# The sample's queries against its states: states as moving operand in four column groups of the array, queries stationary

## The chip, the cores and the metric

One NeuronCore of a Trainium2 chip runs the whole program. The metric is the device time of one execution in microseconds (us); the time of a kernel is the median of its runs. TensorE is called PE in the profile (PEld is its weight load), VectorE DVE, ScalarE ACT, GpSimd POOL, and SyncE SP.

## What is computed

One inference step of a decoder with two layers. Layer 0 mixes by gated linear attention (GLA), layer 1 by a gated short convolution; each layer has an MLP. There are 1024 prompt tokens and a sample of 8 sequences with 4 new tokens each. Only the GLA of the sample is touched. Each of its 8 sequences brings its own state S (128 x 256) for each of 4 heads. Cut to what matters:

```python
def gla_core(q, k, v, g, s0):      # for the sample: one chunk of 4 tokens per sequence
    b = jnp.cumsum(g, axis=3)
    q_dec = q * jnp.exp(b)
    k_dec = k * jnp.exp(-b)
    scores = jnp.where(causal, jnp.einsum('bhnid,bhnjd->bhnij', q_dec, k_dec), 0.0)
    o_intra = jnp.einsum('bhnij,bhnjv->bhniv', scores, v)
    ...
    o_inter = jnp.einsum('bhncd,nbhdv->bhncv', q_dec, s_prev)   # s_prev: the states brought in
    o = o_intra + o_inter
    # new state: decay * s0 + k^T v
```

The new states and the outputs of all tokens are results, in float32.

## The kernel before

The 1056 tokens (1024 of the prompt, then the 32 of the sample) lie along the free axis in three groups of 384, 384 and 288; the sample is the last 32 columns of group 2. The GLA stage runs over 4 heads. In each head: the projections of queries and keys for three token groups, then `core` over nine token tiles (eight of the prompt, and the ninth is the sample), then the gates and the output projection. `proj` (L241) is 24 matmuls that TensorE runs one after the other (8 slices of the contraction, each in three matmuls of high and low parts, L236 to L238). `gated` (L572) takes one `proj`; there are two for each token group. `out(tg)` (L761) is `accumulate` (L252): 8 output blocks of 6 matmuls, each block in a bank of PSUM of its own.

TensorE's order in this stage is that of the code. Work that follows from a step with some delay is put into a list (`after`, L210) with a due time in a planner's clock that counts matmuls (`cost`, L207); `tick` (L221), called at the end of each `proj` and each output block, runs what is due. `need(key)` runs what must be done now. The orders of DVE, ACT and POOL in this stage are made by a scheduler.

PSUM has eight banks here (`ps()`, L81). A new tile takes a bank whose former tile has been read, and TensorE waits for that.

The ninth tile goes to `sample` (L666). Its steps: `outputs` (L672) is due at the first `tick`, that is behind the first `proj` of the gates. For each of two halves m of the 256 value columns it multiplies the sample's values `vt` with the masked scores `sTs`, and then, for each of 8 sequences, a 128 x 128 slice of the state as stationary operand with 4 query columns as moving operand. In float32 each of these matmuls is two instructions on TensorE. ACT copies the result to `o`, and `rms` begins the normalisation. `products` (L685), 800 ns later in the planner's clock, so behind the next `proj`, forms k^T v of the 8 sequences into four banks (`box`): it uses 32 rows of the array at a time, in four row groups. `state(j)` (L693) then adds on DVE, four operations for each j, and a DMA on POOL's queue stores four states; a bank of `box` is free when the operation of `state(1)` on it is done. The buffers of the states (`raw`, three in all) are later filled by the next weights.

The vectors `seq[:, 0]` and `seq[:, 1]` are scalars for each partition, one or zero, that pick for row 32 g + t of a 128-row tile the sequence g or 4 + g.

Of the kernel before, what the change touches and what calls it, by code (L numbers as in the profile page):

```python
# [9 lines left out]
F32 = mybir.dt.float32  # L10
# [3 lines left out]
ALU = mybir.AluOpType  # L14
PSUM = bass.MemoryType.PSUM

P = 128
# [3 lines left out]
NSEQ = 8  # L21
LSEQ = 4
NS = NSEQ * LSEQ
# [5 lines left out]
DV = 256  # L29
# [28 lines left out]
def hybrid_step(ctx, tc, x_prompt, x_sample, state_gla, state_conv, gla_w_in, gla_w_gate_up, gla_b_gate,  # L58
# [4 lines left out]
    V, A, G, PE = nc.vector, nc.scalar, nc.gpsimd, nc.tensor  # L63
# [13 lines left out]
    def nm(s):  # L77
        count[0] += 1
        return f"{s}{count[0]}"

    def ps():  # L81
        return psp.tile([P, 512], F32, tag="ps", name=nm("ps"))

    def ring():
        return ringp.tile([P, RINGW], F32, tag="ring", name=nm("ring"))
# [6 lines left out]
    ident = const.tile([P, P], F32, name="ident")  # L92
# [15 lines left out]
    gconst = glac.enter_context(tc.tile_pool(name="gconst", bufs=1))  # L108
# [39 lines left out]
    seq = gconst.tile([P, 2], F32, name="seq")  # L148
    V.tensor_add(seq, seq1[:, 0, :], seq1[:, 1, :])
    for g in (2, 3):  # L150
        V.tensor_add(seq, seq, seq1[:, g, :])


    units = []
# [52 lines left out]
    def cost(n, passes):  # L207
        clock[0] += passes * (n / PE_GHZ + 3.0)

    def after(key, *steps):  # L210

        later.append([clock[0] + steps[0][0], key, list(steps)])
# [18 lines left out]
    def mm(out, w, x, start=True, stop=True):  # L231
        PE.matmul(out, w, x, start=start, stop=stop)  # L232
        cost(out.shape[-1], 4)
# [170 lines left out]
    start = ctx.enter_context(ExitStack())  # L404
# [56 lines left out]
    with tc.tile_pool(name="gp", bufs=3) as gp:  # L461
# [85 lines left out]
        def rms(h, tg, o):  # L547
            n = TGS[tg][1]
            box = {}

            def squares():
                box["a"], box["b"] = ring(), ring()
                A.activation(box["a"][:, :n], o[:, 0, :n], AF.Square)
                A.activation(box["b"][:, :n], o[:, 1, :n], AF.Square)
                (V if tg == 2 else G).tensor_add(box["a"][:, :n], box["a"][:, :n], box["b"][:, :n])

            def split():
                box["mean"] = mean_over(box["a"], n)

            def var():  # L560
                box["var"] = box["mean"]()

            def norm():
                rstd = rstd_of(box["var"], n, RMS_EPS, D // DV)
                for m in range(2):
                    ncol = col["norm_g"] + h * 2 + m
                    V.scalar_tensor_tensor(o[:, m, :n], o[:, m, :n], par[:, ncol:ncol + 1], rstd[:, :n],
                                           op0=ALU.mult, op1=ALU.mult)

            after(("rms", tg), (300, squares), (1500, split), (1500, var), (500, norm))  # L570
# [17 lines left out]
        def core(h, qkk, uv, dec, o):  # L588
# [77 lines left out]
            def sample(k2t, st, vt):  # L666

                tg, off = 2, 256
                q_ = qkk[tg][0]
                box = []  # L670

                def outputs():  # L672
                    po = ps()
                    for m in range(2):
                        ms = slice(m * P, (m + 1) * P)
                        mm(po[:, m * NS:(m + 1) * NS], vt[:, ms], st, stop=False)
                        for i in range(NSEQ):
                            c = i * LSEQ
                            mm(po[:, m * NS + c:m * NS + c + LSEQ], s0[i // 4][:, i % 4, ms],
                               q_[:, off + c:off + c + LSEQ], start=False, stop=i == NSEQ - 1)  # L680
                    A.copy(o[tg][:, :, off:off + NS], po[:, :2 * NS].rearrange("p (m t) -> p m t", t=NS))
                    rms(h, tg, o[tg])
                    after(("states",), (STEP, products), *[(STEP, lambda j=j: state(j)) for j in range(2)])

                def products():  # L685

                    box.extend(ps() for _ in range(4))
                    for j in range(2):
                        for g in range(4):
                            gs = slice(g * NS, (g + 1) * NS)  # L690
                            mm(box[g][:, j * DV:(j + 1) * DV], k2t[gs, j * P:(j + 1) * P], vt[gs, :])

                def state(j):  # L693
                    for g in range(4):
                        S = s0[j][:, g, :]
                        V.scalar_tensor_tensor(S, S, dec[:, 16 + 4 * j + g:17 + 4 * j + g],
                                               box[g][:, j * DV:(j + 1) * DV], op0=ALU.mult, op1=ALU.add)
                    nc.gpsimd.dma_start(gla_s[0, 4 * j:4 * j + 4, h].rearrange("s p v -> p s v"), s0[j])

                after(("sample",), (0, outputs))  # L700

            s0 = []
            e = early(0)
            vt = values(0)
            for t in range(9):
                if t == 5:
                    for half in range(2):
                        s0.append(raw().rearrange("p (s v) -> p s v", v=DV))
                        nc.gpsimd.dma_start(s0[half],
                                            state_gla[0, half * 4:half * 4 + 4, h].rearrange("s p v -> p s v"))  # L710
                if t < 8:
                    e_next = early(t + 1)
                    vt_next = values(t + 1)
                if t == 7:
                    issue()
                    issue()
                if t < 8:
                    chunks(t, *e, vt)
                    if t == 7:
                        nc.gpsimd.dma_start(gla_p[0, 0, h], state["S"])  # L720
                else:
                    sample(*e, vt)
                if t in (2, 5):
                    rms(h, t // 3, o[t // 3])
                e, vt = e_next, vt_next
# [698 lines left out]
```

## Time and profile before

| | us |
|---|---|
| median of 3 runs (lowest, highest) | 2283.0 (2279.68, 2283.72) |
| the profiled execution | 2281.98 |
| its span, first to last instruction | 2280.3 |
| TensorE busy in it | 2204.7 (97%) |
| DVE, ACT, POOL busy | 1629.4, 1140.2, 520.8 |
| mean granted clock of TensorE | 0.980 of full speed |

The span is the time from the first to the last instruction of the profiled execution; 1.7 us lie around it. Busy shares are averages over the whole span; what a stage waits for is read from that stage. A matmul's shown duration reaches past the start of the next one, since matmuls are pipelined: what one costs in a row of them is the distance between starts.

### The profile page before, as it was taken

To read this page: it belongs to the slowest core of one execution; us is meant where nothing else is said; L and a number is where in the kernel's file an instruction comes from. 1 tells how busy PE (TensorE), PEld (TensorE's weight loads), DVE (VectorE), ACT (ScalarE), POOL (GpSimd) and SP (SyncE) were. 2 spreads that over 40 slices of the span, in tenths; PEclk is the share of its full clock that TensorE was granted. 3 is DMA by queue.
4 is the path that set the end of the run, shared out by engine and by line. 5 is a ranking of instruction groups with operands and counts; after the bars stand their busy time and mean duration, and the time that the engine had idled before them with its cause. 6 is when DMAs were issued, how large, how long until landed. Compare 5 with 4: busy or idle time off the path is not lost.

```text
span 2280.3 us, 43300 instructions
## 1 busy us (share of the span) xinstructions
PE 2204.7 (97%) x17341; PEld 2180.1 (96%) x17341; DVE 1629.4 (71%) x3030; ACT 1140.2 (50%) x2083; POOL 520.8 (23%) x547
## 2 busy tenths in 40 slices
PE   9999999997999999999999999988999999999995
PEld 8999999997999999999999999988999999999995
DVE  7464848466688755588788787987578865578875
ACT  4444435258563436554468454446854344664442
POOL 5102321222312022412102313210332111422121
PEclk9999999998999999999999999999999999999997
DMA  5021212114769356868445657640886544868535
GB/s 163 25 74 40 74 32 65 38 58 108 95 123 222 103 93 130 116 134 205 106 76 85 117 117 129 139 109 19 131 138 158 149 109 102 111 120 207 143 78 136
DMA packets 296326, 249.43 MB, mean 109 GB/s; under 512 B 15316, under 2 KB 238648, under 8 KB 296124
## 3 DMA queue, kind: packets, MB, share of 16 engines
q0 software_dynamic: 122624, 106.53, 30.7%
q1 hardware_dynamic: 173500, 140.13, 20.7%
q8 instruction: 136, 2.23, 0.4%
q14 instruction: 66, 0.54, 0.1%
HBM read 224.91 MB, written 9.12 MB: 103 GB/s over the span
## 4 chain that ended last, share of the span: by engine, by line
PE 89%; DVE 5%; DMA 2%; issue 2%; ACT 1%; POOL 0%; SPq 0%; DVEq 0%; ACTq 0%; POOLq 0%
PE pq L865 67%; PE ps L236 6%; PE ps L237 6%; PE ps L238 6%; PE ps L232 3%; DMA SB<-in_mlp_w_down 1%; PE pq L1170 1%; PE pq L1197 1%; DMA SB<-in_conv_w_out 1%; DVE H L1271 1%; DVE bl L848 0%; DVE wl L848 0%; DVE stats L1153 0%; ACT big L1189 0%; DVE Z L334 0%
## 5 line engine op out<-in xcount | busy, mean ns | idle before, releaser
L865 PE MATMUL pq<-bh,wh 128*128 128x264 f32 x4160 | 846.6, 285 | 9.1 <-ACT bh L847 7.1
L865 PE MATMUL pq<-bl,wh 128*128 128x264 f32 x4160 | 846.9, 284 | 2.6 <-DVE bl L848 2.6
L865 PE MATMUL pq<-bh,wl 128*128 128x264 f32 x4160 | 844.3, 285 | 1.8 <-DVE wl L848 1.7
L865 PEld LDWEIGHTS pq<-bh,wh 128*128 128x128 f32 x4160 | 645.4, 189 | 11.1 <-ACT bh L847 9.3
L865 PEld LDWEIGHTS pq<-bl,wh 128*128 128x128 f32 x4160 | 645.5, 189 | 3.4 <-DVE bl L848 3.1
L865 PEld LDWEIGHTS pq<-bh,wl 128*128 128x128 f32 x4160 | 645.4, 189 | 2.6 <-DVE wl L848 2.4
L847 ACT CAST wh<-raw 128x512 fp32r<-128x512 f32 x312 | 193.6, 621 | 393.1 <-PE pq L865 375.0
L848 DVE TENSOR_TENSOR wl<-raw,wh 128x512 fp32r<-128x512 f32 x312 | 214.2, 687 | 125.9 <-ACT wh L847 124.1
L854 POOL DMA_DIRECT2D SB<-in_mlp_w_up x128 | 163.5, 1332 | 424.1 <-DMA SB<-in_mlp_w_up 251.4
L847 ACT CAST wh<-SB 128x512 fp32r<-128x512 f32 x208 | 128.6, 618 | 239.0 <-PE pq L865 217.6
L848 DVE TENSOR_TENSOR wl<-SB,wh 128x512 fp32r<-128x512 f32 x208 | 142.7, 686 | 87.1 <-ACT wh L847 87.1
L847 ACT CAST bh<-H 128x528 fp32r<-128x528 f32 (+1 forms) x292 | 165.4, 570 | 52.3 <-PE pq L865 46.8
L848 DVE TENSOR_TENSOR bl<-H,bh 128x528 fp32r<-128x528 f32 (+1 forms) x292 | 179.2, 625 | 13.0 <-ACT bh L847 12.6
L854 POOL DMA_DIRECT2D SB<-in_mlp_w_down x96 | 85.0, 1155 | 255.4 <-DVE wl L848 138.4
L236 PE MATMUL ps<-XH,whi 128*128 128x384 f32 (+1 forms) x384 | 128.4, 334 | 0.2 <-ACT XH L401 0.2
L237 PE MATMUL ps<-XL,whi 128*128 128x384 f32 (+1 forms) x384 | 127.4, 332 | 0.3 <-DVE XL L402 0.3
L238 PE MATMUL ps<-XH,wlo 128*128 128x384 f32 (+1 forms) x384 | 127.1, 331 | 0.0
L865 PE MATMUL pq<-bh,rh 128*128 128x264 f32 x320 | 95.5, 299 | 21.8 <-ACT rh L847 12.5
L854 POOL DMA_DIRECT2D SB<-in_conv_w_in x48 | 61.2, 1285 | 170.3 <-DMA SB<-in_conv_w_in 73.1
L865 PE MATMUL pq<-bl,rh 128*128 128x264 f32 x320 | 92.9, 291 | 0.0
L865 PE MATMUL pq<-bh,rl 128*128 128x264 f32 x320 | 92.6, 292 | 0.3 <-DVE rl L848 0.2
L962 ACT ACTIVATE H<-H 128x528 f32<-128x528 f32 x96 | 61.9, 645 | 46.9 <-DVE H L982 27.9
(275 smaller groups left out, 3651.4 us busy)
## 6 DMA issues: line engine op xcount, KB each, us to landing
raw<-in_mlp_w_down SPq DMA_DIRECT2D x160, 256.0 KB, 3.1
SB<-in_mlp_w_up POOLq DMA_DIRECT2D x128, 256.0 KB, 4.8
raw<-in_mlp_w_up SPq DMA_DIRECT2D x96, 256.0 KB, 3.0
SB<-in_mlp_w_down POOLq DMA_DIRECT2D x96, 256.0 KB, 7.9
SB<-in_mlp_w_up SPq DMA_DIRECT2D x64, 256.0 KB, 3.8
raw<-in_gla_w_in SPq DMA_DIRECT2D x24, 512.0 KB, 3.8
SB<-in_conv_w_in POOLq DMA_DIRECT2D x48, 256.0 KB, 4.7
raw<-SB POOLq DMA_DIRECT2D x36, 256.0 KB, 4.1
```

The source lines that it names most:

```text
L232: PE.matmul(out, w, x, start=start, stop=stop)
L236: PE.matmul(out, wh, xh, start=first, stop=False)
L237: PE.matmul(out, wh, xl, start=False, stop=False)
L238: PE.matmul(out, wl, xh, start=False, stop=last)
L847: A.copy(hi[:, :w], src)
L848: V.tensor_sub(lo[:, :w], src, f32(hi[:, :w]))
L854: queue.dma_start(dst, src, **kw)
L865: PE.matmul(out[:, c:c + NT], w, b[:, n * NT:(n + 1) * NT], start=first and i == 0, stop=last and i == 2)
L962: A.activation(h, h, AF.Relu, scale=sign)
L1170: PE.transpose(pt[:tn, k * P:(k + 1) * P], z[:, k, t0:t0 + tn], ident)
L1197: PE.transpose(pt[:, k * P:k * P + tn], box["y"][:tn, k * P:(k + 1) * P], ident[:tn, :tn])
L1271: V.scalar_tensor_tensor(o, i, w[k], o, op0=ALU.mult, op1=ALU.add)
```

## The change

`outputs` is split in two steps. `inter` takes the place where `outputs` stood: for each half j of the sequences and each g of four it multiplies the 32 query columns of all sequences (stationary, 128 x 32) with the state of sequence 4 j + g (moving, 128 x 256); the result goes to partitions 32 g to 32 g + 31, so each g has a group of 32 columns of the array. Each result row has then a token's query against one sequence's state; only one of eight is wanted. DVE picks it: one operation multiplies the first half by `seq[:, 0]`, a second adds the other half times `seq[:, 1]`. The result x has, in its 128 rows, the 32 tokens four times, with zeros where the row group isn't the token's sequence. `outputs`, 2000 ns later in the planner's clock, takes for each m the product of `vt` and `sTs` as before, and adds x to it by one matmul with `rep4`, which adds up the four row groups. `rep4` is made at the start by six small operations on DVE.

```diff
+    rep4 = gconst.tile([P, P], F32, name="rep4")
+    r4 = rep4[:, 0:NS]
+    V.tensor_add(r4, ident[:, 0:NS], ident[:, NS:2 * NS])
+    for g in (2, 3):
+        V.tensor_add(r4, r4, ident[:, g * NS:(g + 1) * NS])
+    for g in (1, 2, 3):
+        V.tensor_copy(rep4[:, g * NS:(g + 1) * NS], r4)
...
+                def inter():
+
+                    pi = ps()
+                    for j in range(2):
+                        for g in range(4):
+                            PE.matmul(pi[g * NS:(g + 1) * NS, j * DV:(j + 1) * DV], q_[:, off:off + NS], s0[j][:, g, :],
+                                      start=True, stop=True)
+                    cost(DV, 8)
+                    x = ring()[:, :DV]
+                    V.tensor_scalar(x, pi[:, 0:DV], seq[:, 0:1], None, op0=ALU.mult)
+                    V.scalar_tensor_tensor(x, pi[:, DV:2 * DV], seq[:, 1:2], x, op0=ALU.mult, op1=ALU.add)
+                    box.append(x)
+
                 def outputs():
+                    x = box.pop()
                     po = ps()
                     for m in range(2):
                         ms = slice(m * P, (m + 1) * P)
                         mm(po[:, m * NS:(m + 1) * NS], vt[:, ms], st, stop=False)
-                        for i in range(NSEQ):
-                            c = i * LSEQ
-                            mm(po[:, m * NS + c:m * NS + c + LSEQ], s0[i // 4][:, i % 4, ms],
-                               q_[:, off + c:off + c + LSEQ], start=False, stop=i == NSEQ - 1)
+                        mm(po[:, m * NS:(m + 1) * NS], x[:, ms], rep4[:, 0:NS], start=False)
...
-                after(("sample",), (0, outputs))
+                after(("sample",), (0, inter), (2000, outputs))
```

On TensorE, in head 0, this stands before between the first and the second `proj` of the gates (`g` are the queries, `raw` the states, `ring ... ones_r` the end of what came ahead; x4 means four in a row):

```order
L309 MATMUL ps_1268<-ring_1202,ones_r 128x384
L310 MATMUL ps_1268<-ring_1203,ones_r 128x384
L232 MATMUL ps_1271<-sTs,vt_1197 128x32
L232 MATMUL ps_1271<-g_605,raw_1025 128x4 x4
L232 MATMUL ps_1271<-g_605,raw_1027 128x4 x4
L232 MATMUL ps_1271<-sTs,vt_1197 128x32
L232 MATMUL ps_1271<-g_605,raw_1025 128x4 x4
L232 MATMUL ps_1271<-g_605,raw_1027 128x4 x4
L236 MATMUL ps_1298<-XH_92,whi_685 128x384
```

In the changed program the same place, between the two projections, reads:

```order
L317 MATMUL ps_1275<-ring_1209,ones_r 128x384
L318 MATMUL ps_1275<-ring_1210,ones_r 128x384
L685 MATMUL ps_1278<-raw_1032,g_612 32x256 x4
L685 MATMUL ps_1278<-raw_1034,g_612 32x256 x4
L244 MATMUL ps_1297<-XH_92,whi_692 128x384
```

and behind the second `proj`, where `products` stood before, TensorE now has `outputs` and the gate of the next head:

```order
L240 MATMUL ps_1334<-sTs,vt_1204 128x32
L240 MATMUL ps_1334<-rep_135,ring_1287 128x32
L240 MATMUL ps_1334<-sTs,vt_1204 128x32
L240 MATMUL ps_1334<-rep_135,ring_1287 128x32
L492 MATMUL ps_1347<-gl_377,w_gate 128x384
```

So 18 matmuls have become 8 and 4, and `products` has moved behind the third `proj`: one `proj` lies between it and `out(0)` instead of two. The last rows ahead of the third bank that `out(0)` takes are now the following (head 0; `ring ... ones_r` are the sums of squares of the sample's group):

```order
L246 MATMUL ps_1462<-g_1343,wlo_1225 128x384
L317 MATMUL ps_1470<-ring_1433,ones_r 128x288
L318 MATMUL ps_1470<-ring_1434,ones_r 128x288
L244 MATMUL ps_1473<-g_1293,whi_1215 128x384
```

That sum stood ahead of the first block of `out(0)` before, and stands now behind its second. On DVE the operations of `state` (here L715, L696 before; `ps_1389` to `ps_1392` are the four banks) stand in head 0 as follows, behind the last gated operand that `out(0)` needs (L593, L585 before):

```order
L593 TENSOR_TENSOR g_1345<-ring_1340,g_1343 128x384
L715 SCALAR_TENSOR_TENSOR raw_1032<-raw_1032,dec_467,ps_1389 128x256
L715 SCALAR_TENSOR_TENSOR raw_1032<-raw_1032,dec_467,ps_1390 128x256
L715 SCALAR_TENSOR_TENSOR raw_1032<-raw_1032,dec_467,ps_1391 128x256
L502 TENSOR_TENSOR ring_1352<-ring_1352,ring_1349 128x384
L563 TENSOR_TENSOR ring_1384<-ring_1384,ring_1385 128x288
L506 SCALAR_TENSOR_TENSOR b_1357<-reset,ring_1352 128x384
L312 CAST ring_1433<-ring_1384 128x288
L715 SCALAR_TENSOR_TENSOR raw_1032<-raw_1032,dec_467,ps_1392 128x256
L313 TENSOR_TENSOR ring_1434<-ring_1384,ring_1433 128x288
L589 TENSOR_TENSOR ring_1401<-o_697,ring_1401 128x384
L715 SCALAR_TENSOR_TENSOR raw_1034<-raw_1034,dec_467,ps_1389 128x256
```

Before, the first of them stood ahead of that operand, in the middle of a normalisation, and the others lay further apart; the fifth is the first that frees a bank. The orders of SP and POOL are as before, but for one addition of POOL in head 2.

## Rows read from the trace of the kernel before

**Rows 1.** The page's chain that ended last: shares by engine.

```profile
PE 89%; DVE 5%; DMA 2%; issue 2%; ACT 1%; POOL 0%; SPq 0%; DVEq 0%; ACTq 0%; POOLq 0%
```

**Rows 2.** Stretches: length, busy PE, PEld, DVE, ACT, POOL; clock, DMA share, GB/s.

```profile
110.00:200.00 90.00, 90.00 (x621) 88.69 (x620) 53.70 (x129) 34.84 (x67) 10.78 (x17) 1.00 0.20 59
```

**Rows 3.** Timeline of PE, head 1, `outputs` to `products`: start, duration, line, operands.

```profile
217.58 0.30 PE L232 MATMUL ps<-sTs,vt 128*128 128x32 f32 x2
217.72 1.93 PE L232 MATMUL ps<-g,raw 128*128 128x4 f32 x16
219.50 0.39 PE L232 MATMUL ps<-sTs,vt 128*128 128x32 f32 x2
...
221.51 0.42 PE L236 MATMUL ps<-XH,whi 128*128 128x384 f32 x1
...
222.84 0.52 PE L237 MATMUL ps<-XL,whi 128*128 128x384 f32 x1
223.16 0.52 PE L238 MATMUL ps<-XH,wlo 128*128 128x384 f32 x1
...
226.28 0.34 PE L236 MATMUL ps<-XH,whi 128*128 128x384 f32 x1
...
227.15 0.34 PE L238 MATMUL ps<-XH,wlo 128*128 128x384 f32 x1
227.42 1.15 PE L232 MATMUL ps<-vt,ring 32*128 32x256 f32 x16
```

**Rows 4.** Timeline of PE: first rows of `outputs` and `products`, heads 0, 2, 3.

```profile
96.42 0.30 PE L232 MATMUL ps<-sTs,vt 128*128 128x32 f32 x2
...
107.86 1.15 PE L232 MATMUL ps<-vt,ring 32*128 32x256 f32 x16
108.94 0.45 PE L484 MATMUL ps<-gl,w_gate 96*128 96x384 f32 x1
...
337.58 0.30 PE L232 MATMUL ps<-sTs,vt 128*128 128x32 f32 x2
...
347.43 1.15 PE L232 MATMUL ps<-vt,ring 32*128 32x256 f32 x16
...
459.39 0.30 PE L232 MATMUL ps<-sTs,vt 128*128 128x32 f32 x2
...
470.87 1.15 PE L232 MATMUL ps<-vt,ring 32*128 32x256 f32 x16
```

**Rows 5.** Stretches as in rows 2: inside `low_rank`, and around 221.51, head 1.

```profile
28.00:32.00 4.00, 4.00 (x26) 2.53 (x25) 3.90 (x6) 1.56 (x2) 4.00 (x3) 1.00 0.62 188
220.00:224.00 4.00, 4.00 (x26) 4.00 (x27) 1.31 (x3) 2.59 (x6) 0.00 (x0) 0.85 0.00 0
```

**Rows 6.** Groups of PE, 25 to 36 us; timeline of PEld, the sample's values.

```profile
L473 PE MATMUL ps<-XH,wg 128*32 128x384 f32 x16 | 5.4, 338 | 0.0
...
89.96 0.11 PEld L237 LDWEIGHTS ps<-wlo,XH 128*32 128x32 f32 x1
90.07 0.11 PEld L238 LDWEIGHTS ps<-whi,XL 128*32 128x32 f32 x1
```

**Rows 7.** Timeline of DVE, program's start and head 0; in brackets idle time.

```profile
5.81 2.50 DVE L402 TENSOR_TENSOR XL<-ps,XH 128x512 fp32r<-128x512 f32 x4 [2.68 <-ACT XH L401]
...
99.16 0.15 DVE L191 TENSOR_SCALAR wmean<-wmean 128x1 f32<-128x1 f32 x1 [0.48 <-ACT whi L190]
```

**Rows 8.** Timeline of DVE, head 0, among the operations of `state`.

```profile
114.62 0.87 DVE L696 SCALAR_TENSOR_TENSOR raw<-raw,dec,ps 128x256 f32<-128x256 f32 x2
115.41 0.55 DVE L494 TENSOR_TENSOR ring<-ring,ring 128x384 f32<-128x384 f32 x1
115.88 0.47 DVE L696 SCALAR_TENSOR_TENSOR raw<-raw,dec,ps 128x256 f32<-128x256 f32 x1
116.27 0.95 DVE L498 TENSOR_TENSOR_SCAN b<-reset,ring 128x384 f32<-128x384 bf16 x1
```

**Rows 9.** Timeline of PE, head 2, the first matmul of `out(0)`.

```profile
359.20 0.44 PE L236 MATMUL ps<-g,whi 128*128 128x384 f32 x1 [1.29 <-DVE raw L696]
```

## The prediction

> **What bounds the kernel now.** I read the chain that ended last first, since it says whose work sets the end: TensorE holds 89% of it, DVE 5% [rows 1]. Then the stretches of the GLA stage, since the change lies only there: from 110 to 200 us TensorE is busy for 90.00 of 90.00 us, at the full clock (1.00), while DVE works 53.70 us and ACT 34.84 us [rows 2]. So in this stage a microsecond taken off TensorE is a microsecond off the end, as long as no other engine or buffer becomes late; and work given to DVE is free as long as nobody waits for it.
>
> Then the timeline of TensorE at the place itself. In head 1 the step `outputs` starts at 217.58 and the next `proj` at 221.51: 3.93 us for 36 instructions [rows 3]. Sixteen of them take from 217.72 to 219.50, that is 0.111 us each, with only 4 columns moving. The reader should look at what comes after: the matmuls of the next `proj` start 0.174 us apart at the end of it (226.28 to 227.15, five steps), but 0.32 us apart at 222.84 to 223.16 [rows 3]. The granted clock in that stretch is 0.85 on the mean [rows 5]: TensorE fell from 2.4 to 1.2 GHz and came back. Before the fall it ran the 4-column instructions, without idle time. So the step costs twice: its own 3.93 us, and the slow matmuls behind it.
>
> The whole price is read from the first row of `outputs` to the first row of `products`, since the same work lies between these in every head: 11.44 us in head 0 (96.42 to 107.86), 9.84 in head 1, 9.85 in head 2, 11.48 in head 3 [rows 3, 4]. Together 42.6. At the full clock it would be 3.93 for the step, 24 x 0.174 = 4.18 for the `proj`, and some 0.15 for the two changes between kinds of matmul (0.10 of it is seen ahead of 227.42, which comes 0.27 behind 227.15) [rows 3]: 8.26 a head, 33.0 for four. The falls of the clock cost 42.6 - 33.0 = 9.6 us.
>
> **Part 1: the 4-column matmuls go.** 36 instructions of 3.93 us a head leave, and in their place come 16 instructions of `inter` and 8 of the new `outputs`. The 8 have 32 columns moving; the two `sTs` instructions of that size take 0.14 (217.58 to 217.72), the 4-column ones 0.111 each; at the larger, 8 x 0.111 = 0.89, and 0.1 for entering: 1.0 us.
>
> The trace has no four column groups. Nearest from below are the 16 instructions of `products`, also float32 and 256 wide, in four row groups: 107.86 to 108.94, 1.08 us [rows 4], and 0.2 for entering and leaving: 1.3. If the groups didn't run beside each other, each instruction would cost a 256-column pass alone or two. Loads of 128 x 32 follow each other every 0.11 us where 256 columns move in one pass [rows 6]; float32 in two passes would be 0.22, so 16 x 0.22 = 3.5, and with 0.2 for entering and leaving 3.7. I take 1.3: same size, same number of passes, and also four parts of one array that don't share a result. The step then costs 2.3 instead of 3.93: 1.7 us less with the shorter entry of the next `proj`, 6.8 for four heads.
>
> Here a rule speaks against the change. What the rows show: 128 x 32 loads of one and the same column group run every 0.11 us, one for each matmul that moves 256 columns, so a load does overlap a running matmul in the same rows [rows 6]. The Trainium skill, page "TensorE: Matmul & The Clock Gate", section "Part 3: Packing small matmuls — row/col tiling", says that a weight load overlaps running matmuls only where their row groups differ. Column groups all have the same rows, so by that rule the 16 would run in turn, at the 3.7 us. The trace disagrees for one group, and shows nothing of four. The table of the same section has a gain of 2.38 times for three column tiles, so the page itself leaves it open.
>
> **Part 2: the clock.** Does it still fall? 32 columns of weights with a long moving operand stand in `low_rank`: 16 instructions of 128 x 384 on one operand, as many on the other, in one row behind each other, and the clock of that stretch is 1.00 [rows 5, 6]. `inter` is of that kind or denser, and only the 8 small ones (0.9 us a head instead of 3.93) resemble what was taken away. I take the falls as gone: -9.6. The other end is that they stay, 0.
>
> This is the place of the second rule. What the rows show: no row between 217.58 and 222.84 has idle time ahead of it, and yet the clock falls [rows 3]. The Trainium skill, same page, section "Why this matters for your kernels", names idle gaps between bursts as what drops the clock. By that rule the small matmuls weren't the cause, and the falls would stay; the trace speaks against it, since all four lie behind the same step.
>
> **Part 3: what is added beside TensorE.** DVE has two operations of 128 x 256 from PSUM a head, near 0.47 each [rows 8]. Who waits: `outputs`, one `proj` after `inter`, that is 4.2 us later. Queued between the two on DVE are `wmean`, which waits for ACT (in head 0 it ran at 99.16, 2.7 us behind the step's start [rows 4, 7]), and a 384-wide operation of about 0.55. The second then ends about 2.7 + 0.15 + 0.55 + 0.47 = 3.9 us behind the start of `inter`, and TensorE asks at 1.3 + 4.2 = 5.5. Slack 1.6, cost nothing; without that cover at most the difference. The six operations that make `rep4` are of some 0.15 each; DVE is idle 2.68 us there [rows 7]: nothing. One more bank (`pi`) and one more buffer are held for about 4 us.
>
> **Part 4: what moves.** `outputs` and `products` come one `proj` later in the program, so `state` and the two stores behind it on POOL's queue do too, and behind those the two loads of the next head's weights, on SP's queue. In absolute time TensorE arrives some 4 us earlier at everything, so they start about when they did. The banks are the tighter point. TensorE reaches the third block of `out(0)` 4.2 (`proj`) + 12 x 0.175 + 0.35 = 6.6 us behind `products`, and that block takes the bank which the fifth `state` operation frees. On DVE, from the first to the fifth, there are five of these (0.40 to 0.47), one scan (0.87 to 0.95), two of 384 (0.47 to 0.55), and three of 288 columns, no longer than those [rows 8]: 5 x 0.43 + 0.9 + 2 x 0.5 + 3 x 0.4 = 5.3 us. So 1.3 us of slack in heads 0 and 1, if ACT delivers in time. In head 2 the centring adds work on DVE, and there TensorE waits already: 1.29 us for `state` [rows 9]. I take +0.5 for all heads. The ends are -1.3 (that wait goes) and +12.6 (one `proj` of 4.2 us in each of three heads, if the operations of `state` come that much later).
>
> **The sum.** -6.8 - 9.6 + 0.5 = -15.9 us. Against the profiled execution: 2281.98 - 15.9 = 2266.1. That execution lies 1.0 below the median, so the median should be 2267.
>
> **The rivals.**
> *The groups run in turn.* Then the step costs 3.7 + 1.0 = 4.7, 0.8 more than now, +3.1 for four heads; with the clock kept: 2281.98 + 3.1 - 9.6 + 0.5 = 2276, median 2277. For it: nothing in the trace runs in column groups; against: row groups do run together. The first rule above gives this time too.
> *The change doesn't do what it says to the clock.* Groups together, falls as before: -6.8 + 0.5, median 2276.7. For it: the 8 small instructions are left; against: the full clock of the 32-column stretch [rows 5, 6]. The second rule above gives this time too.
> *Banks.* `state` late by up to a `proj` in heads 0 to 2: -15.9 - 0.5 + 12.6 = -3.8, median 2279, no change.
> *Slower: groups in turn, and the clock falls.* 3.7 us on a quarter of the columns in each head, followed by a `proj` at half clock as in heads 0 and 3, which lost 3.2 us each where heads 1 and 2 lost 1.6: +3.1, and 4 x 3.2 - 9.6 = +3.2 for longer falls, +0.5: median 2290. It decides from the point where `inter` takes more than 2.9 us (then the step is no shorter than before) and the clock is at half speed behind it.
>
> **How the numbers follow.** Forecast 0.60 (2267, by itself 2261 to 2272 with partly joint groups and the spread of runs, 2279.68 to 2283.72); in turn 0.13; falls stay 0.11; banks 0.09; slower 0.07. A measurement of this kernel can tell about 0.2%, 4.6 us, from no change: faster means below 2278.4. The first three lie there, though the second and third come within 2 us of it, and some of the fourth: 0.60 + 0.10 + 0.08 + 0.03 = 0.81. Same 0.12, slower 0.07. The range reaches down to 2260 (the wait of head 2 gone, `inter` at its best) and up to 2278, so that it takes in both middle cases.
>
> **What would show it.** Right: in each head `inter` lasts 1.0 to 1.4 us on TensorE, the `proj` behind it has starts 0.174 apart, from the first row of `inter` to the first of `outputs` 5.5 us; the granted clock is 1.00 there; no wait of TensorE for `seq` operations on DVE. Wrong: starts in `inter` 0.2 us apart; starts of 0.32 us behind `inter` or `outputs`; a wait of TensorE for `state` at the third block of `out(0)` in heads 0 and 1, or over 2 us in head 2; or a gain in this stage that isn't found in the time at the end.

## The result, and the profile after

The changed kernel takes 2267.7 us in the median of 4 runs (2264.55 to 2269.15), beside 2281.3 for the kernel before in the same comparison (2275.76 to 2283.72): ratio 0.9942, 95% interval 0.9928 to 0.9955. A second set of runs of the same changed kernel gave 0.9927 (0.9914 to 0.9941). The forecast was 2267, range 2260 to 2278. The profiled execution took 2264.55 us, the lowest of its four, with a span of 2262.8 us and a mean granted clock of 0.986 (0.980 before).

The page of the kernel after: busy time by engine, and the chain that ended last. TensorE's share of the chain hardly changed [rows 1]; the stage is still bound by it.

```profile
PE 2187.5 (97%) x17293; PEld 2159.4 (95%) x17293; DVE 1632.2 (72%) x3044; ACT 1134.8 (50%) x2080; POOL 521.1 (23%) x547
...
PE 88%; DVE 5%; DMA 2%; issue 2%; ACT 2%; POOL 0%; DVEq 0%; ACTq 0%; POOLq 0%
```

Stretches of the kernel after (columns as in [rows 2]): 110 to 200 us as before, and two that hold the step in all four heads. The clock is 1.00 in all; before it was 0.85 behind the step of head 1 [rows 5].

```profile
110.00:200.00 90.00, 90.00 (x635) 88.50 (x634) 51.87 (x128) 31.64 (x68) 12.42 (x20) 1.00 0.20 59
90.00:290.00 200.00, 200.00 (x1385) 194.73 (x1384) 129.19 (x289) 90.21 (x165) 37.18 (x46) 1.00 0.22 65
290.00:490.00 200.00, 198.17 (x1413) 191.30 (x1412) 128.39 (x281) 90.25 (x182) 42.41 (x57) 1.00 0.16 50
```

Timeline of TensorE, kernel after, head 0 (start, duration, line, operands). L685 is `inter`, L244 to L246 `proj`, L240 the two products of `outputs`:

```profile
95.12 0.34 PE L318 MATMUL ps<-ring,ones_r 128*128 128x384 f32 x1
95.39 1.07 PE L685 MATMUL ps<-raw,g 128*32 128x256 f32 x16
96.39 0.44 PE L244 MATMUL ps<-XH,whi 128*128 128x384 f32 x1
96.67 0.34 PE L245 MATMUL ps<-XL,whi 128*128 128x384 f32 x1
96.84 0.34 PE L246 MATMUL ps<-XH,wlo 128*128 128x384 f32 x1
...
100.48 0.34 PE L246 MATMUL ps<-XH,wlo 128*128 128x384 f32 x1
100.66 0.30 PE L240 MATMUL ps<-sTs,vt 128*128 128x32 f32 x2
100.80 0.39 PE L240 MATMUL ps<-rep,ring 128*128 128x32 f32 x2
101.02 0.39 PE L240 MATMUL ps<-sTs,vt 128*128 128x32 f32 x2
101.24 0.39 PE L240 MATMUL ps<-rep,ring 128*128 128x32 f32 x2
101.47 0.42 PE L492 MATMUL ps<-gl,w_gate 96*128 96x384 f32 x1
```

The 16 instructions of `inter` take 1.00 us (95.39 to 96.39), the 8 of `outputs` 0.81 (100.66 to 101.47): 1.81 where the step took 3.93 [rows 3]. Behind `inter` the starts of `proj` lie 0.17 apart, not 0.32. From `inter` to `outputs` it is 5.27 us, with no wait.

One wait of TensorE is new. Timeline of the kernel after, head 2 (in brackets idle time and releaser):

```profile
348.19 0.41 PE L317 MATMUL ps<-ring,ones_r 128*128 128x288 f32 x1 [1.54 <-DVE raw L715]
...
355.66 0.40 PE L244 MATMUL ps<-XH,whi 128*128 128x288 f32 x1 [0.28 <-ACT ring L300]
```

The 1.54 us wait is for the bank that the operations of `state` free; it stands at the sum of squares between the second and the third block of `out(0)`. The wait of before at the first matmul of `out(0)` [rows 9] is gone.

Where the time went, from the first row of the step in one head to that in the next (the last stretch ends at the first matmul of the MLP, whose rows before and after stand first):

```profile
529.10 1.69 PE L865 MATMUL pq<-bh,wh 128*128 128x264 f32 x6 [6.93 <-ACT bh L847]
...
511.79 1.69 PE L884 MATMUL pq<-bh,wh 128*128 128x264 f32 x6 [6.93 <-ACT bh L866]
```

| stretch | before | after | less |
|---|---|---|---|
| start to head 0 | 96.42 | 95.39 | 1.03 |
| head 0 to 1 | 121.16 | 116.08 | 5.08 |
| head 1 to 2 | 120.00 | 116.58 | 3.42 |
| head 2 to 3 | 121.81 | 119.25 | 2.56 |
| head 3 to MLP | 69.71 | 64.49 | 5.22 |

The sum at the first matmul of the MLP is 17.3 us, at the end 17.5: between these two profiles all of it arises ahead of the MLP, and nothing is given back later. The 17.5 us belong to these two executions, the one after being the fastest of its four: the medians differ by 13.7 us here and by 15.6 in the second set.

### The profile page after: what moved, and what is told of

Read it like the earlier page. It is cut to its first block, busy times and chain, and to the rows that moved or that the text cites. A ratio compares the mean times of both kernels' runs of the same rounds, so it can differ in the third digit from the quotient of the medians.

```text
span 2262.8 us, 43216 instructions
## 1 busy us (share of the span) xinstructions
PE 2187.5 (97%) x17293; PEld 2159.4 (95%) x17293; DVE 1632.2 (72%) x3044; ACT 1134.8 (50%) x2080; POOL 521.1 (23%) x547
## 3 DMA queue, kind: packets, MB, share of 16 engines
q8 instruction: 135, 2.21, 0.4%
## 4 chain that ended last, share of the span: by engine, by line
PE 88%; DVE 5%; DMA 2%; issue 2%; ACT 2%; POOL 0%; DVEq 0%; ACTq 0%; POOLq 0%
PE pq L884 68%; PE ps L244 6%; PE ps L245 5%; PE ps L246 5%; PE ps L240 2%; DMA SB<-in_mlp_w_down 1%; PE pq L1189 1%; PE pq L1216 1%; DMA SB<-in_conv_w_out 1%; DVE H L1290 1%; DVE bl L867 0%; DVE wl L867 0%; DVE stats L1172 0%; ACT big L1208 0%; DVE Z L342 0%
## 5 line engine op out<-in xcount | busy, mean ns | idle before, releaser
L244 PE MATMUL ps<-XH,whi 128*128 128x384 f32 (+1 forms) x384 | 125.1, 326 | 0.5 <-ACT ring L300 0.3
L246 PE MATMUL ps<-XH,wlo 128*128 128x384 f32 (+1 forms) x384 | 123.3, 321 | 0.0
```

The costliest lines, as they stand in the source:

```text
L244: PE.matmul(out, wh, xh, start=first, stop=False)
L246: PE.matmul(out, wl, xh, start=False, stop=last)
```

## The experiments

The theory: the old step cost its own time and, by falls of the clock, the time of the matmuls in or behind it; four column groups run beside each other. The rivals are the prediction's. For every kernel the table has the time from the first row of the step to the first of `products` in the four heads, and from the first row of the step in head 0 to the MLP. In the first four kernels one `proj` lies between these two rows; in `e1`, the change and `e2` two; in `e3` one.

| kernel | heads 0 to 3 | to the MLP | ratio of the runs |
|---|---|---|---|
| before | 11.44, 9.84, 9.85, 11.48 | 432.68 | |
| before, second profile (`f1`) | 9.85, 9.86, 9.87, 8.28 | 427.97 | |
| 32 columns moving (`f2`) | 8.29, 9.88, 11.47, 9.87 | 428.02 | 0.9983 |
| no state term (`f3`) | 4.72, 4.71, 4.70, 4.73 | 410.29 | 0.9909 |
| step in halves (`e1`) | 12.66, 12.62, 12.66, 12.47 | 427.17 | 0.9977 |
| the change | 10.60, 10.63, 10.60, 10.45 | 416.40 | 0.9942 |
| the change again | 10.61, 10.63, 10.60, 10.45 | 416.61 | 0.9927 |
| one column group (`e2`) | 13.17, 13.20, 13.19, 13.04 | 424.40 | 0.9964 |
| `products` early (`e3`) | 6.17, 6.20, 6.17, 6.17 | 415.46 | 0.9931 |

### Clock alone: the old step in two halves

```diff
+                    half(1)
+                    po = box.pop()
...
-                after(("sample",), (0, outputs))
+                after(("sample",), (0, lambda: half(0)), (2000, outputs))
```

`half(m)` is the body of the old loop over m, into one shared bank; one `proj` stands between the halves, and `products` comes one `proj` later, as in the change.

> The kernel before with its 36 instructions of a head kept, cut into two halves of 18 with one projection of 4.2 us between them; what follows moves back by one projection, as in the change. Theory (the clock falls behind a dense stretch of 4-column matmuls; half a stretch of 2.0 us among full projections doesn't do it): granted clock 1.00 at all four places, starts of 0.174 us behind both halves, and 9.6 us less than before, less some 0.5 for the moved steps: ratio to before 0.996. Rival (the falls come with these matmuls however they are spread, or with something else at this place): starts of 0.32 us behind a half in most heads, ratio 0.999 to 1.001.

Measured: 2276.3 us, ratio 0.9977 (0.9967 to 0.9987). At all four places the clock stays at full speed. Stretches (head 0 to behind the step of head 2), and TensorE's timeline at the two halves of head 0:

```profile
90.00:230.00 140.00, 140.00 (x988) 136.95 (x987) 80.75 (x182) 66.61 (x124) 15.64 (x25) 1.00 0.18 55
230.00:373.00 143.00, 140.00 (x970) 136.61 (x968) 101.16 (x213) 62.56 (x117) 38.67 (x46) 1.00 0.22 65
```

```profile
94.92 0.30 PE L232 MATMUL ps<-sTs,vt 128*128 128x32 f32 x2
95.06 1.93 PE L232 MATMUL ps<-g,raw 128*128 128x4 f32 x16
96.85 0.43 PE L236 MATMUL ps<-XH,whi 128*128 128x384 f32 x1
97.11 0.34 PE L237 MATMUL ps<-XL,whi 128*128 128x384 f32 x1
...
101.13 0.30 PE L232 MATMUL ps<-sTs,vt 128*128 128x32 f32 x2
101.27 1.93 PE L232 MATMUL ps<-g,raw 128*128 128x4 f32 x16
103.06 0.42 PE L484 MATMUL ps<-gl,w_gate 96*128 96x384 f32 x1
```

At the step of head 3 it is 1.00 as well (455 to 466 us). The same 36 instructions at the same 0.11 us each, only parted, were followed by no fall in this profile. In heads 0, 1 and 3 the gain against before is 3.09, 1.52 and 3.22 us, the falls that the prediction had read there (3.2, 1.6, 3.2). But head 2 is 2.32 us longer than before, so the whole is about half of the 9.6. Its waits there:

```profile
354.86 0.44 PE L236 MATMUL ps<-g,whi 128*128 128x384 f32 x1 [1.24 <-DVE Z L266]
...
373.23 0.53 PE L309 MATMUL ps<-ring,ones_r 128*128 128x288 f32 x1 [2.00 <-DVE ring L304]
373.56 0.52 PE L236 MATMUL ps<-g,whi 128*128 128x384 f32 x1
373.88 0.52 PE L237 MATMUL ps<-g,whi 128*128 128x384 f32 x1
```

So in head 2 TensorE waits for operations of DVE, and behind the 2.00 us wait the clock falls (starts 0.32 apart). Whether they are late because TensorE no longer loses time ahead of them, or because what follows the step stands one `proj` later here, this run doesn't part.

### Do the groups run together? All in one column group

```diff
-                            PE.matmul(pi[g * NS:(g + 1) * NS, j * DV:(j + 1) * DV], q_[:, off:off + NS], s0[j][:, g, :],
+                            PE.matmul(pi[0:NS, j * DV:(j + 1) * DV], q_[:, off:off + NS], s0[j][:, g, :],
...
-                    V.tensor_scalar(x, pi[:, 0:DV], seq[:, 0:1], None, op0=ALU.mult)
-                    V.scalar_tensor_tensor(x, pi[:, DV:2 * DV], seq[:, 1:2], x, op0=ALU.mult, op1=ALU.add)
+                    V.memset(x, 0.0)
+                    V.tensor_scalar(x[0:NS], pi[0:NS, 0:DV], seq[0:NS, 0:1], None, op0=ALU.mult)
+                    V.scalar_tensor_tensor(x[0:NS], pi[0:NS, DV:2 * DV], seq[0:NS, 1:2], x[0:NS], op0=ALU.mult, op1=ALU.add)
```

> The changed kernel with the eight matmuls of inter all in the first group of 32 columns, so that they can only run in turn; the part of the sample's output that comes from the states is left out for most sequences. Theory (the four groups run together in the changed kernel, 1.00 us for 16 instructions): starts 0.21 to 0.22 us apart, inter 3.4 to 3.6 us, the clock stays at 1.00 as in low_rank, so 2.5 us more in each head and 10 us more in all than the changed kernel: ratio to before 0.998 to 0.999. Rival 1 (the groups gain nothing): no slower than the changed kernel, 0.994. Rival 2 (a quarter of the columns at work lets the clock fall): starts of 0.32 us behind inter, 6 to 13 us on top, ratio 1.001 to 1.004.

Measured: 2273.5 us, ratio 0.9964 (0.9950 to 0.9978). Timeline of TensorE, head 0:

```profile
95.26 3.64 PE L685 MATMUL ps<-raw,g 128*32 128x256 f32 x16
...
98.83 0.44 PE L244 MATMUL ps<-XH,whi 128*128 128x384 f32 x1
99.11 0.34 PE L245 MATMUL ps<-XL,whi 128*128 128x384 f32 x1
```

In turn, the 16 take 3.57 us, or 0.223 each; beside each other they took 1.00. (All 16 write the same 32 partitions of PSUM here; these go with the column group, so the two aren't parted.) From step to step the change gains 2.58 us by the groups in heads 0, 1 and 3 (up to `products` 13.17 against 10.60). In head 2 only 0.26 of that is seen, since the waits of 1.54 and 0.28 us aren't there when TensorE comes later; so the ratio lies below the 0.998 that was expected from 2.5 us in each head. The clock stays at full speed behind 3.57 us on a quarter of the columns (1.00 from 90 to 290 and from 290 to 490 us).

### Products early

```diff
-                    after(("states",), (STEP, products), *[(STEP, lambda j=j: state(j)) for j in range(2)])
+                    products()
+                    after(("states",), *[(STEP, lambda j=j: state(j)) for j in range(2)])
```

> The changed kernel with products put directly behind outputs, so that two projections lie between it and the output projection again, as before the change. Theory (the wait of 1.5 us in head 2 is for a bank that state holds because products came one projection later): state starts 4.2 us earlier, the wait in head 2 goes, 1.0 to 1.5 us less than the changed kernel, ratio to before 0.9935 against 0.994. Rival (the wait in head 2 belongs to the centring on DVE, as the 1.3 us of the kernel before did): the wait stays at 1 to 1.5 us and the time is that of the changed kernel within 0.05%.

Measured: 2265.1 us, ratio 0.9931 (0.9918 to 0.9943). It can't be told from the change. In the trace the wait for `state` in head 2 is gone, and two smaller ones stand in its place, 0.48 us for an addition of DVE to the residual stream (a bank of `out` itself) and 0.74 for ACT:

```profile
353.08 0.44 PE L244 MATMUL ps<-g,whi 128*128 128x384 f32 x1 [0.48 <-DVE Z L274]
...
355.32 0.40 PE L244 MATMUL ps<-XH,whi 128*128 128x288 f32 x1 [0.74 <-ACT ring L300]
```

From the step of head 2 to that of head 3 0.82 us remain of the gain (118.43 against 119.25), less than the 1.0 to 1.5 that was expected. So the new wait is that of the banks, as the prediction's Part 4 has it, and is worth less than it lasts.

### The change once more

> The changed kernel once more, in more rounds beside the kernel before on one chip. Theory (5.4 us from fewer instructions and 9 to 10 from the clock, the same in every run): ratio 0.993 to 0.9945, and a span shorter by 15 to 17 us. Rival (part of the 17 us between the two profiles is the clock's chance at the start of the program): ratio nearer to 0.9945 to 0.9955.

Measured: 2266.4 us, ratio 0.9927 (0.9914 to 0.9941). No fall of the clock in the four heads, and the wait of head 2 is 1.65 us. At the first matmul of the MLP this profile is 16.6 us ahead of that of before (512.51 against 529.10), at its end 14.4. Behind the GLA stage its clock fell at two places more than in the first profile of the change (0.86 on the mean from 1448 to 1456 and from 2224 to 2236 us, 1.00 there in the first); why isn't shown.

### The kernel before once more

> The kernel before once more, for a second profile of it. Theory: the 1.0 us that the profile of before lost ahead of 96.42 us belong to that execution alone (a fall of the clock between 8 and 16 us), and not to the change; then this profile has its first row of `outputs` in head 0 near 95.4, and the four stretches from `outputs` to `products` again sum to 41 to 44 us, with a fall of the clock behind each of the four. Rival: the change made the start faster; then the first row of `outputs` is again at 96.2 or later.

Measured: one run of 2277.9 us, and it missed on both points. The start came at 96.42 again, and only three of the four places had a fall, of 1.6 us each: the stretches sum to 37.86. Timeline of TensorE in head 3 of this profile, where there was none:

```profile
457.89 0.30 PE L232 MATMUL ps<-sTs,vt 128*128 128x32 f32 x2
458.03 1.93 PE L232 MATMUL ps<-g,raw 128*128 128x4 f32 x16
459.82 0.39 PE L232 MATMUL ps<-sTs,vt 128*128 128x32 f32 x2
460.04 1.93 PE L232 MATMUL ps<-g,raw 128*128 128x4 f32 x16
461.83 0.42 PE L236 MATMUL ps<-XH,whi 128*128 128x384 f32 x1
...
465.90 0.34 PE L238 MATMUL ps<-XH,wlo 128*128 128x384 f32 x1
466.17 1.15 PE L232 MATMUL ps<-vt,ring 32*128 32x256 f32 x16
```

The stretch is 8.28 us here, where the prediction had worked out 8.26 for the full clock. So the falls cost 0, 1.6 or 3.2 us a head, differently in each execution: together 9.5 us in the first profile, 4.7 in the second.

As for the start: the clock fell between 8 and 16 us in before, `f1` and `f3` (first row of the step at 96.42, 96.42, 97.31). It didn't in `e1` and `f2`, whose start has the same instructions (94.92, 95.14), nor in the four profiles with `rep4` (95.26 to 95.90). The 1.03 us are thus not needed for the change's account; whether `rep4` makes that fall rarer stays open. Among the starts without the fall those with `rep4` are the later ones, by 0.1 to 1.0 us, so that it costs nothing isn't shown either.

### Few columns, or many weights? 32 columns moving

```diff
-                            mm(po[:, m * NS + c:m * NS + c + LSEQ], s0[i // 4][:, i % 4, ms],
-                               q_[:, off + c:off + c + LSEQ], start=False, stop=i == NSEQ - 1)
+                            PE.matmul(po[:, m * NS:(m + 1) * NS], s0[i // 4][:, i % 4, ms],
+                               q_[:, off:off + NS], start=False, stop=i == NSEQ - 1)
+                            cost(LSEQ, 4)
```

> The kernel before, but each of the 64 matmuls of `outputs` on a slice of a state moves all 32 query columns instead of its sequence's 4, so the sample's outputs hold the sum over all states; the number of instructions, their weights and their order stay. Theory A, the fall comes from how few columns move in a row of instructions that are paced by their weights: at 0.11 us an instruction as before (the step again 3.9 us), but with eight times the columns the clock keeps 1.00 behind the step, the stretch from `outputs` to `products` is 8.3 to 8.6 us in each head, and the time falls by 9.6 us (ratio 0.996). Theory B, the fall comes from the change of the stationary operand at each instruction, however many columns move: the falls stay, the stretches sum to 41 to 44 us, and the ratio is 0.999 to 1.001.

Measured: 2277.7 us, ratio 0.9983 (0.9973 to 0.9992). Head 0 had no fall, the others did; timeline of TensorE in head 1, and its stretch:

```profile
213.15 0.30 PE L232 MATMUL ps<-sTs,vt 128*128 128x32 f32 x2
213.29 1.95 PE L679 MATMUL ps<-g,raw 128*128 128x32 f32 x16
215.07 0.39 PE L232 MATMUL ps<-sTs,vt 128*128 128x32 f32 x2
215.30 2.17 PE L679 MATMUL ps<-g,raw 128*128 128x32 f32 x16
217.28 0.67 PE L236 MATMUL ps<-XH,whi 128*128 128x384 f32 x1
217.75 0.52 PE L237 MATMUL ps<-XL,whi 128*128 128x384 f32 x1
```

```profile
216.00:220.00 4.00, 4.00 (x21) 4.00 (x21) 1.40 (x3) 2.48 (x4) 0.00 (x0) 0.61 0.00 0
```

Eight times the columns cost the same 0.11 us an instruction, and the falls come all the same, here already inside the step. Theory A is refuted: moving 32 columns didn't keep the clock at 1.00. The stretches sum to 39.5 us, where A had 33 to 34 and B 41 to 44, and the ratio lies a little under theory B's. The sum is within what `f1` showed of the chance in a fall (37.86); the ratio is over ten runs and its interval ends at 0.9992, so that falls are rarer or shorter with 32 columns isn't ruled out. What B says of the cause isn't shown by this: `inter`, too, loads new weights for each instruction, though the same queries, and only 32 columns of them. What the profiles have together is that 36 instructions of 0.11 us with 128 x 128 weights in a row had a fall in or behind them at 10 of 12 places (before, `f1`, `f2`), and 18 of them, or `inter`, or `e2`'s 3.57 us with its long moving operand, at none of 24.

### The bound: no state term

```diff
-                        mm(po[:, m * NS:(m + 1) * NS], vt[:, ms], st, stop=False)
-                        for i in range(NSEQ):
...
+                        mm(po[:, m * NS:(m + 1) * NS], vt[:, ms], st)
+                        cost(NSEQ * LSEQ, 4)
```

> The kernel before without the 64 matmuls of `outputs` on the states (the states' part of the sample's outputs is left out, and nothing is put in its place): a bound on what any form of this step can give. Theory: the step shrinks from 3.93 to 0.4 us and the clock never falls, so 14.1 + 9.6 = 23.7 us less, and 1 to 4 us of it given back at the operations of DVE in head 2: ratio 0.990 to 0.992, and the stretch from `outputs` to `products` 4.6 to 4.9 us in heads 0, 1 and 3. Rival, the falls come from something else at that place: 14 us less, ratio 0.994, and the stretch 6.5 us or more.

Measured: 2260.0 us, ratio 0.9909 (0.9892 to 0.9925). Timeline of TensorE, head 0:

```profile
97.31 0.53 PE L232 MATMUL ps<-sTs,vt 128*128 128x32 f32 x4
97.67 0.42 PE L236 MATMUL ps<-XH,whi 128*128 128x384 f32 x1
```

The step is 0.36 us, the clock keeps full speed, and the waits in head 2 are 2.02 us for `state` and 0.38 for DVE. From the step to the MLP it takes 410.29 us, the change 416.40. Of these 6.1 us the two new steps are 4 x (1.81 - 0.36) = 5.8. So the change has 16.3 of the 22.4 us that leaving out the states' part brings, counted from the first profile of before; counted from the second (427.97) it has 11.6 of 17.7.

## Why the prediction was right

Its sum for the GLA stage was -15.9 us; the trace has 432.68 - 416.40 = 16.3. The rest of the profiles' difference is the start (1.0) and 0.2 behind the stage. The mechanism was right; that the sum came within 0.4 us is partly luck, since two sizes were off in opposite directions: the step gave 0.9 us more in the four heads than its term, and the wait for a bank took 0.4 more. The steps one by one:

- **TensorE bounds the stage.** Right: between the two profiles what left it is found at the end, us for us.
- **Part 1, the step.** Right in kind, the term was too small: 3.93 to 1.81 us, where 2.3 was taken. The priced row, 1.08 us for `products` in row groups [rows 4], was a good neighbour for four column groups (1.00), and `outputs` took 0.81, not 1.0. The 0.2 for the changes between kinds of matmul is there: `inter` starts 0.27 behind the row ahead of it (95.12 to 95.39), not 0.17, and one more such change stands behind `outputs`. That leaves 2.12 - 0.2 = 1.9 a head. With the falls taken off, heads 0, 1 and 3 are 1.9, 1.9 and 2.0 us shorter (5.08 - 3.16, 3.42 - 1.56, 5.22 - 3.20), where 1.7 was forecast.
- **The groups in turn.** The rival is refuted by `e2`, which builds it: 3.57 us, where the prediction had worked out 3.5 for this rival [rows 6], and 2273.5 us, where it had 2277 (in head 2 the added time only took the place of the wait). In the change the same 16 pass in 1.00 us. The Trainium skill, page "TensorE: Matmul & The Clock Gate", section "Part 3: Packing small matmuls — row/col tiling", says that a load overlaps only where row groups differ, and has a table with 2.38 times for three column tiles. The trace goes with the table and not with the rule: 3.57 times for four column groups, all on the same rows.
- **Part 2, the clock.** Right: no fall in any of the four heads, in either profile of the change, and `e1` gave back the falls' price in heads 0, 1 and 3 with the instructions of the step unchanged (in head 2 waits took its place). What the prediction missed is that the price is a draw, and that in heads 0 and 3 the fall began inside the step and not behind it (the second sixteen instructions took 2.21 us in head 0, from 98.57 to 100.78, and 3.27 in head 3, from 461.54 to 464.81, in place of 1.78). It read 9.6 from one execution; another had 4.7. From the second profile the same working would have given -6.8 - 4.7 + 0.5 = -11 us: against that execution's own 2277.9 again 2267, and with the prediction's last step, up to the median of before (2281.1 in that comparison, 3.2 more), 2270. Since the sum was made against the time of the execution in which the falls were read, the draw would have moved the forecast by 3 us, inside its range. The gain against the median of before hangs on it fully, 15.9 or 11, and the runs of before (2275.5 to 2285.2 over all comparisons) are spread by more than the 4.8 us between these two.
- **Idle gaps as the cause.** The rival that the falls stay is refuted. At 10 places the clock fell with no idle time ahead, and behind the waits of 1.24 to 2.02 us in head 2 it fell only once, behind the 2.00 us of `e1`. The Trainium skill's section "Why this matters for your kernels" on that page names idle gaps between bursts of matmuls. That fits the fall ahead of the MLP, where TensorE waits 9.5 us (before, 516 to 520 us: TensorE busy 0.00 us, clock 0.54), but not these 10.
- **Part 3, DVE.** Right: no wait. Timeline of DVE, kernel after, head 0:

```profile
96.52 0.48 DVE L689 TENSOR_SCALAR ring<-ps,seq 128x256 f32<-128x256 f32 x1 [3.88 <-PE ps L685]
96.92 0.14 DVE L199 TENSOR_SCALAR wmean<-wmean 128x1 f32<-128x1 f32 x1
96.98 0.55 DVE L297 TENSOR_SCALAR ring<-ps 128x384 f32<-128x384 f32 x1
97.45 0.48 DVE L690 SCALAR_TENSOR_TENSOR ring<-ps,seq,ring 128x256 f32<-128x256 f32 x1
```

  The second operation ends at 97.93, 2.5 us behind the first row of `inter`, where 3.9 was estimated; `wmean` didn't wait for ACT in this head. TensorE asks at 100.66: slack 2.7 instead of 1.6.
- **Part 4, the banks.** The place was right, the third block of `out(0)` in head 2, and heads 0 and 1 had no wait. The size was 1.54 us there, in place of 1.29 elsewhere [rows 9]. Head 2 gained 2.56 - 1.57 = 1.0 us where the others gained 1.9, so the term is +0.9, and +0.5 was taken.

## What to carry to other kernels

Read the price of a step of many small matmuls from its first row to the first row of a fixed later mark, not from its own duration: here the clock's falls in and behind it cost 9.5 us in one execution and 4.7 in another, beside the 15.7 of the four steps. Take that price from more than one execution when it varies. Here many small slices of state made the better moving operand: with few query columns stationary in separate column groups, the results selected on an engine that isn't the bottleneck and added up by one more small matmul for each half, 36 instructions of 3.93 us became 24 of 1.81. And when TensorE gets faster ahead of a place where it already waited, expect part of the gain there to turn into the next wait (apart from the falls, head 2 gave 1.0 us and the others 1.9).

## What the runs showed of the hardware

- Sixteen float32 instructions of 128 x 32 weights and 256 moving columns took 1.00 us in four column groups and 3.57 in one.
- With 128 x 128 weights changed at every instruction, 4 and 32 moving columns cost the same: 16 in 1.78 us (213.29 to 215.07 in `f2`) and 1.79 (458.03 to 459.82 in `f1`).
- TensorE's granted clock fell from 2.4 to 1.2 GHz in or behind 36 such instructions in a row at 10 of 12 places, without idle time ahead, and behind none of the eight runs of 18 in `e1`. Whether a place has a fall, and of 1.6 or 3.2 us, changes from one execution to the next. What in these instructions brings it about is open; with 32 moving columns in place of 4 there were falls too, at three of four places.
